# Head norms of a hybrid decoder layer: sums in quarters of the array, one root over all tokens, one product per head to spread it

## The chip, the core and the metric

The kernel runs on one core of a Trainium2 chip. A core has five engines that run side by side, each through its own list of instructions in order: TensorE (PE, with its weight loads shown apart as PEld), VectorE (DVE), ScalarE (ACT), GpSimd (POOL) and SyncE (SP, here the issuer of most DMAs). Matmul results land in PSUM, all else lives in SBUF; both have 128 partitions. The metric is the device time of one execution in microseconds (us), the median of several runs.

## The reference, cut to what matters

One decoder layer for 1024 prompt tokens and 8 sequences of 4 sample tokens: an RG-LRU branch and a gated linear attention (GLA) branch with four heads of 256 values, merged, then a SwiGLU network. What the change touches is the norm of each GLA head's output, per token, over its 256 features:

```python
o, S_T = _gla_chunked(q, k, v, g, S0)
o = o * lax.rsqrt(jnp.mean(o * o, axis=-1, keepdims=True) + EPS) * gla_norm_g.reshape(GLA_HEADS, GLA_DV)
y_b = o.reshape(B, T, GLA_DV_TOTAL) * jax.nn.silu(u_r)
m = jax.nn.sigmoid(u_ga) * (y_a @ proj_a) + jax.nn.sigmoid(u_gb) * (y_b @ proj_b)
```

All data are float32.

## The kernel before

Activations lie with features on the partitions and tokens along the free axis. The tokens are done in two halves, A (512 prompt tokens) and B (512 prompt tokens and the 32 sample tokens, 544 columns). The big products are made in float32r with each operand split in a high and a low part: `gemm` issues three matmuls per 128 features (L355, L356, L357), on pieces of 512 columns in A and of 272 in B. Weights come by DMA, are rounded to the high part on ScalarE (L136) and get their low part on VectorE (L137). Small products are plain float32 matmuls.

PSUM has two pools. `ax` (two banks) serves everything small: transposes, the sums of the norms, scores, the spreading of a norm's root. `mm` (six banks) takes the big products: six tiles of one bank in A, three of two banks in B. In SBUF the tags that matter here are "S" (17 buffers of 1088 columns) and "t" (6 buffers of 544 columns, made by `T`).

The four heads are done in two pairs. `gla(pr, ...)` makes a pair's attention: it begins with an Exp and a Ln on ScalarE (L635, L636), a scan on VectorE (L641), Exps (L646, L654), two multiplications on GpSimd (L647, L655), then masked scores (L663, L664) and seven levels of decay (L694 to L725), and ends with the squares of the pair's two heads (L839) and the sum of a head's two feature tiles into `oac` (L841), one 128 x 544 tile for each head, still to be summed over the partitions.

`head_norm(pr)` follows. In the kernel before it makes the sum over the partitions with `ssq_mm` (L362): for every 128 tokens one matmul whose stationary operand is the 128 x 128 piece of `oac` and whose moving operand is a single column of ones, so tokens come out on partitions: four pieces for each head in A, five in B. `rsqrt` (L278 to L285) computes the root on VectorE in eleven tiny instructions on 8 or 10 columns: an integer guess and three Newton steps. `spread` (L374) brings the root back along the free axis and onto all partitions, with one float32 matmul for each 128 tokens (the root's column repeated as the stationary operand, the identity as the moving one); ScalarE copies it to SBUF (L377, L379) and VectorE multiplies the head by it (L859). `y_b_tiles` (L878) and `merge_b` use the result.

The order of the work: generators yield the TensorE time of what they emit, in us, and `mix(main, fill)` emits from `fill` until it has given what `main` asked for. The emission order is a priority; a planner in the framework then fixes the order on each engine by its own estimates of durations and by when buffers come free. `head_norm(0)` runs inside `side(gla(1), head_norm(0))`: one step of it is emitted with each step of the second pair's attention, and its own yields are not used. `head_norm(1)` runs after that attention with its yields (6, 3, 3) filled from the RG-LRU branch (`lru`). In half A, chunks of the conditioning product (`ada`, L194) are woven into the fill as well; they split a product over the four 32-column quarters of the array, the way the change does:

```python
for g in range(4):
    pe.matmul(ps[32 * g:32 * g + 32, c:c + 256], cth[:, 4 * (k % 2) + g, :], raw[:, g * 256:(g + 1) * 256],
```

There are four calls of `head_norm`: A0 and A1 (half A, pairs 0 and 1), B0 and B1.

Of the kernel before, what the change touches and what calls it, by code (L numbers as in the profile page):

```python
# [7 lines left out]
F32 = mybir.dt.float32  # L8
F32R = mybir.dt.float32r
I32 = mybir.dt.int32  # L10
AF = mybir.ActivationFunctionType
OP = mybir.AluOpType
# [3 lines left out]
P = 128  # L16
# [10 lines left out]
CHUNKS = ([(0, HP)], [(0, 272), (272, 272)])  # L27
LEVELS = (64, 32, 16, 8, 4, 2, 1)
EPS = 1e-6
EARLY = 4  # L30
AHEAD = 70
def starts_of(w):
    return [min(i, w - P) for i in range(0, w, P)]
# [9 lines left out]
def bc(ap, shape):  # L43
    return ap.to_broadcast(shape)
# [3 lines left out]
def hybrid_layer(ctx, tc, I, O):  # L48
    nc = tc.nc
    pe, act, dve, pool, sp = nc.tensor, nc.scalar, nc.vector, nc.gpsimd, nc.sync  # L50
# [11 lines left out]
    cp = ctx.enter_context(tc.tile_pool(name="cp", bufs=1))  # L62
# [4 lines left out]
    tp = ctx.enter_context(tc.tile_pool(name="tp", bufs=6))  # L67
    axp = ctx.enter_context(tc.tile_pool(name="axp", bufs=2, space=PSUM))

    def S(name, dt=F32):  # L70
        return sbig.tile([P, 2 * 544], dt, tag="S", name=name)

    def T(name, w=544):
        return tp.tile([P, w], F32, tag="t", name=name)
# [15 lines left out]
    def ax(name):  # L90
        return axp.tile([P, 512], F32, tag="ax", name=name)
# [6 lines left out]
    ident = cp.tile([P, P], F32, name="ident")  # L98
# [7 lines left out]
        for t, src in (lmask, "lmask"), (bmask, "bmask"), (hlru0, "slru"), (sconv, "sconv"):  # L106
            sp.dma_start(t, I[src])
    wa2 = cp.tile([P, NH, P], F32R, name="wa2")
    ones = cp.tile([P, 1], F32, name="ones")
    pool.memset(ones, 1.0)  # L110
    rmask = cp.tile([P, 544], F32, name="rmask")
    pool.memset(rmask, 1.0)
    pool.memset(rmask[:, 0:HP:P], 0.0)
# [135 lines left out]
    def derive():  # L249
        wraw = S("wa2raw")  # L250
        w3 = wraw[:, :NH * P].rearrange("p (h m) -> p h m", m=P)
        pool.dma_start(w3, I["wa2"])
        act.activation(wa2, w3, AF.Copy)
        dve.tensor_sub(wa2[96:112], w3[96:112], wa2[96:112].bitcast(F32))
        dve.tensor_scalar_mul(vh[:, 0:20], vec[:, V_BA:V_BA + 20], 0.5)
        dve.tensor_scalar_mul(vh[:, 20:28], vec[:, V_GN:V_GN + 8], 0.5)
        lam = vec[:, V_LAM:V_LAM + NR]
        dve.scalar_tensor_tensor(lw[:, 0], lam, -1.0, lam, op0=OP.mult, op1=OP.min)
        act.activation(lw[:, 1], lw[:, 0], AF.Exp)
        dve.tensor_scalar_add(lw[:, 2], lw[:, 1], 2.0)  # L260
        dve.reciprocal(lw[:, 2], lw[:, 2])
        dve.tensor_mul(lw[:, 1], lw[:, 1], lw[:, 2])
        dve.tensor_mul(lw[:, 2], lw[:, 1], lw[:, 1])
        dve.memset(lw[:, 3], 1.0 / 17.0)
        for kk in range(7, -1, -1):
            dve.tensor_mul(lw[:, 3], lw[:, 3], lw[:, 2])
            dve.tensor_scalar_add(lw[:, 3], lw[:, 3], 1.0 / (2 * kk + 1))
        dve.tensor_mul(lw[:, 3], lw[:, 3], lw[:, 1])
        dve.tensor_scalar(lw[:, 4], lam, -1.0, 0.0, op0=OP.mult, op1=OP.max)
        dve.scalar_tensor_tensor(lw[:, 5], lw[:, 3], 2.0, lw[:, 4], op0=OP.mult, op1=OP.add)  # L270
        dve.tensor_scalar_mul(sp4, lw[:, 5], -4.0)


    def rsqrt(dst, ssq, n, scale, name):
        w = cp.tile([P, 3, 16], F32, name="rs_" + name, tag="rs", bufs=2)
        a, t = w[:, 0, :n], w[:, 1, :n]
        yi = cp.tile([P, 16], I32, name="ri_" + name, tag="ri", bufs=2)
        dve.tensor_scalar(a, ssq, scale, EPS, op0=OP.mult, op1=OP.add)  # L278
        dve.tensor_scalar(yi[:, :n], a.bitcast(I32), -0.5, float(0x5F3759DF), op0=OP.mult, op1=OP.add)
        y = yi[:, :n].bitcast(F32)  # L280
        for it in range(3):
            dve.scalar_tensor_tensor(t, a, -0.5, y, op0=OP.mult, op1=OP.mult)
            dve.tensor_mul(t, t, y)
            o = dst if it == 2 else w[:, 2, :n]
            dve.scalar_tensor_tensor(o, t, 1.5, y, op0=OP.add, op1=OP.mult)  # L285
            y = o
# [29 lines left out]
    class Half:  # L316
# [42 lines left out]

        def ssq_mm(s, ps, src, starts, col0, first, last):  # L360
            for i, o in enumerate(starts):
                pe.matmul(ps[:, col0 + i:col0 + i + 1], src[:, o:o + P], ones,  # L362
                          start=(first and i == 0), stop=(last and i == len(starts) - 1), skip_group_check=True)


# [477 lines left out]
            s.oacc = accs  # L843

        def head_norm(s, pr):
            n, N, accs = f"{s.n}{pr}", s.N, s.oacc
            os_ = s.os_[2 * pr:2 * pr + 2]
            starts = starts_of(N)
            nt = len(starts)
            ps = ax("ops" + n)  # L850
            for i in range(2):
                s.ssq_mm(ps, accs[i], starts, i * nt, i == 0, i == 1)
            rstd = cp.tile([P, 10], F32, name="orstd" + n, tag="orstd", bufs=2)
            rsqrt(rstd[:, :2 * nt], ps[:, :2 * nt], 2 * nt, 1.0 / 256, "o" + n)
            yield 6
            for i in range(2):
                rb = s.spread(rstd[:, i * nt:(i + 1) * nt], N, f"o{n}{i}")
                o3 = os_[i][:, :2 * N].rearrange("p (v n) -> p v n", v=2)
                dve.tensor_mul(o3, o3, bc(rb[:, :N].unsqueeze(1), [P, 2, N]))  # L859
                yield 3  # L860

        def r_tiles(s):
            N = s.N
# [342 lines left out]
    A.begin()  # L1206
    load_later()
    derive()
    A.branches(None)
    up1 = A.ffn1(1)  # L1210
# [115 lines left out]
```

## Time and profile before

| | us |
|---|---|
| median of 3 runs | 2040.42 (2039.70 to 2045.27) |
| the profiled execution, own time | 2041.18 |
| its span, first to last instruction | 2039.2 |
| TensorE busy | 2005.9 |
| VectorE busy | 1096.8 |
| ScalarE busy | 799.0 |
| GpSimd busy | 76.1 |

The mean granted TensorE clock of the profiled execution was 0.996. The time outside the span is 2.0 us. In a timeline, a row shows the start, the duration, the engine and line, and what was written from what; a matmul's duration includes its pipeline, so its cost is read from one row's start to the next row's start. A float32 matmul leaves two records, a float32r matmul one.

### The profile page before, as it was taken

To read this page: it belongs to the slowest core of one execution; us is meant where nothing else is said; L and a number is where in the kernel's file an instruction comes from. 1 tells how busy PE (TensorE), PEld (TensorE's weight loads), DVE (VectorE), ACT (ScalarE), POOL (GpSimd) and SP (SyncE) were. 2 spreads that over 40 slices of the span, in tenths; PEclk is the share of its full clock that TensorE was granted. 3 is DMA by queue.
4 is the path that set the end of the run, shared out by engine and by line. 5 is a ranking of instruction groups with operands and counts; after the bars stand their busy time and mean duration, and the time that the engine had idled before them with its cause. 6 is when DMAs were issued, how large, how long until landed. Compare 5 with 4: busy or idle time off the path is not lost. (4 is left out here: it accounts for less than half of the span.)

```text
span 2039.2 us, 31760 instructions
## 1 busy us (share of the span) xinstructions
PE 2005.9 (98%) x13306; PEld 1808.0 (89%) x13306; DVE 1096.8 (54%) x1768; ACT 799.0 (39%) x1117; POOL 76.1 (4%) x130
## 2 busy tenths in 40 slices
PE   8999999999999999999999999999999999999997
PEld 5887877777899888888899999999999999999997
DVE  5647586544358433446473597764334773333346
ACT  3534375533335322333352355653322442222232
POOL 0101001000000000000010011010000000000000
PEclk9999999999999999999999999999999999999998
DMA  8323223334344323232412312323233542232243
GB/s 305 105 92 125 88 94 116 102 119 159 93 153 158 124 78 119 93 132 84 149 63 87 126 53 94 109 89 104 73 92 108 177 134 87 72 105 93 82 121 123
DMA packets 74638, 228.39 MB, mean 112 GB/s; under 512 B 8704, under 2 KB 16768, under 8 KB 74496
## 3 DMA queue, kind: packets, MB, share of 16 engines
q1 hardware_dynamic: 71536, 217.38, 32.8%
q0 software_dynamic: 2416, 8.44, 1.1%
q8 instruction: 104, 1.70, 0.3%
q10 hardware_dynamic: 544, 0.56, 0.1%
q14 instruction: 38, 0.31, 0.0%
HBM read 217.11 MB, written 9.23 MB: 111 GB/s over the span
## 5 line engine op out<-in xcount | busy, mean ns | idle before, releaser
L357 PE MATMUL f3psb<-fab,f3b_hl 128*128 128x272 f32 x352 | 101.4, 288 | 0.0
L355 PE MATMUL f3psb<-fab,f3b_hl 128*128 128x272 f32 x352 | 101.3, 288 | 0.0
L356 PE MATMUL f3psb<-fab,f3b_hl 128*128 128x272 f32 x352 | 100.9, 287 | 0.0
L136 ACT ACTIVATE f3b_hl<-f3b_raw 128x768 fp32r<-128x768 f32 (+1 forms) x45 | 35.7, 793 | 88.6 <-PE f3psb L357 58.3
L355 PE MATMUL f3psa<-faa,f3a_hl 128*128 128x512 f32 x176 | 68.7, 390 | 0.0
L357 PE MATMUL f3psa<-faa,f3a_hl 128*128 128x512 f32 x176 | 68.5, 389 | 0.0
L356 PE MATMUL f3psa<-faa,f3a_hl 128*128 128x512 f32 x176 | 68.5, 389 | 0.0
L355 PEld LDWEIGHTS f3psb<-fab,f3b_hl 128*128 128x128 f32 x352 | 66.4, 189 | 0.0
L357 PEld LDWEIGHTS f3psb<-fab,f3b_hl 128*128 128x128 f32 x352 | 66.2, 188 | 0.0
L356 PEld LDWEIGHTS f3psb<-fab,f3b_hl 128*128 128x128 f32 x352 | 66.1, 188 | 0.0
L137 DVE TENSOR_TENSOR f3b_hl<-f3b_raw,f3b_hl 128x768 fp32r<-128x768 f32 (+1 forms) x45 | 40.1, 892 | 35.2 <-ACT f3b_hl L136 34.8
L136 ACT ACTIVATE f3a_hl<-f3a_raw 128x768 fp32r<-128x768 f32 (+1 forms) x32 | 25.4, 793 | 84.3 <-PE f3psa L357 47.9
L137 DVE TENSOR_TENSOR f3a_hl<-f3a_raw,f3a_hl 128x768 fp32r<-128x768 f32 (+1 forms) x32 | 28.5, 892 | 39.1 <-ACT f3a_hl L136 38.4
L355 PE MATMUL uxpsb<-h1b,uxpsb_hl 128*128 128x272 f32 x160 | 47.0, 293 | 0.1
L357 PE MATMUL uxpsb<-h1b,uxpsb_hl 128*128 128x272 f32 x160 | 46.4, 290 | 0.0
L355 PE MATMUL ugpsb<-h1b,ugpsb_hl 128*128 128x272 f32 x160 | 46.2, 289 | 0.0
L357 PE MATMUL ugpsb<-h1b,ugpsb_hl 128*128 128x272 f32 x160 | 46.1, 288 | 0.0
L356 PE MATMUL uxpsb<-h1b,uxpsb_hl 128*128 128x272 f32 x160 | 45.9, 287 | 0.0
L356 PE MATMUL ugpsb<-h1b,ugpsb_hl 128*128 128x272 f32 x160 | 45.8, 286 | 0.0
L357 PEld LDWEIGHTS f3psa<-faa,f3a_hl 128*128 128x128 f32 x176 | 33.0, 188 | 7.0 <-DVE f3a_hl L137 0.2
L356 PEld LDWEIGHTS f3psa<-faa,f3a_hl 128*128 128x128 f32 x176 | 33.0, 188 | 6.9
L355 PEld LDWEIGHTS f3psa<-faa,f3a_hl 128*128 128x128 f32 x176 | 33.0, 188 | 6.8
(1477 smaller groups left out, 7129.0 us busy)
## 6 DMA issues: line engine op xcount, KB each, us to landing
ada<-in_ada_w SPq DMA_DIRECT2D x48, 512.0 KB, 5.3
f3b_raw<-in_ffn SPq DMA_DIRECT2D x23, 384.0 KB, 3.1
f3b_raw<-in_ffn SPq DMA_DIRECT2D x22, 320.0 KB, 2.9
woa_raw<-in_w_out SPq DMA_DIRECT2D x13, 512.0 KB, 3.5
wob_raw<-in_w_out SPq DMA_DIRECT2D x13, 512.0 KB, 3.2
f3a_raw<-in_ffn SPq DMA_DIRECT2D x16, 384.0 KB, 3.1
uxpsa_raw<-in_w_in SPq DMA_DIRECT2D x10, 512.0 KB, 3.6
ugpsa_raw<-in_w_in SPq DMA_DIRECT2D x10, 512.0 KB, 3.6
```

The lines of the kernel that those rows point to most:

```text
L136: act.activation(hl[:, 0, :n], raw[:, :n], AF.Copy)
L137: dve.tensor_sub(hl[:, 1, :n], raw[:, :n], hl[:, 0, :n].bitcast(F32))
L355: pe.matmul(out, wh, x[:, o:o + w], start=st, stop=False)
L356: pe.matmul(out, wh, x[:, N + o:N + o + w], start=False, stop=False)
L357: pe.matmul(out, wl, x[:, o:o + w], start=False, stop=en)
```

## The change

The sum is turned around: a 128 x 32 block of ones is the stationary operand, and `oac` moves through the array, so the sum comes out with tokens along the free axis and repeated on 32 partitions. Four such matmuls fill the four quarters of the array: quarters 0 and 2 hold head 0, quarters 1 and 3 hold head 1. In B the 544 columns are two chunks of 272, each with an `ax` tile of its own. The root is then computed on all partitions and tokens: Ln and Exp with scale -0.5 on ScalarE give the first guess, two Newton steps follow on VectorE. The result is rounded to float32r on ScalarE, and partitions 64 to 127 get the low part. One float32r matmul for each head and chunk, with a stationary operand that picks a head's high row and low row (`pick`), adds the two parts and spreads them over all partitions. Copy and multiplication stay. `head_norm` yields 9, 1.5 and 1.5.

The new tiles: `eps` and `pick` (small constants), "on" (a buffer of tag S, with the mean square and the root), "ot" and "or" (two buffers of tag t), and in B a second `ax` tile for the sums. `ones` grows to 32 columns, and the other norms use its first column.

```diff
-    ones = cp.tile([P, 1], F32, name="ones")
+    ones = cp.tile([P, 32], F32, name="ones")
...
+    pick = cp.tile([P, 2], F32R, name="pick")
...
+        dve.tensor_add(pick, ident[:, 0:33:32], ident[:, 64:97:32])
...
-            for i in range(2):
-                s.ssq_mm(ps, accs[i], starts, i * nt, i == 0, i == 1)
-            rstd = cp.tile([P, 10], F32, name="orstd" + n, tag="orstd", bufs=2)
-            rsqrt(rstd[:, :2 * nt], ps[:, :2 * nt], 2 * nt, 1.0 / 256, "o" + n)
-            yield 6
+            chunks = CHUNKS[s.hf]
+            wt = S("on" + n)
+            a, y = wt[:, :N], wt[:, 544:544 + N]
+            pss = []
+            for ci, (o, w) in enumerate(chunks):
+                ps = ax(f"ops{n}{ci}")[:, :w]
+                for g in range(4):
+                    pe.matmul(ps[32 * g:32 * g + 32], ones, accs[g % 2][:, o:o + w], start=True, stop=True, skip_group_check=True)
+                pss.append(ps)
+            for ps, (o, w) in zip(pss, chunks):
+                act.activation(y[:, o:o + w], ps, AF.Ln, scale=1.0 / 256, bias=eps)
+                dve.tensor_scalar(a[:, o:o + w], ps, 1.0 / 256, EPS, op0=OP.mult, op1=OP.add)
+            act.activation(y, y, AF.Exp, scale=-0.5)
+            t = T("ot" + n)[:, :N]
+            for it in range(2):
+                dve.scalar_tensor_tensor(t, a, -0.5, y, op0=OP.mult, op1=OP.mult)
+                dve.tensor_mul(t, t, y)
+                dve.scalar_tensor_tensor(y, t, 1.5, y, op0=OP.add, op1=OP.mult)
+            r = tp.tile([P, 544], F32R, tag="t", name="or" + n)
+            act.activation(r[:, :N], y, AF.Copy)
+            dve.tensor_sub(r[64:, :N], y[64:], r[64:, :N].bitcast(F32))
+            yield 9
             for i in range(2):
-                rb = s.spread(rstd[:, i * nt:(i + 1) * nt], N, f"o{n}{i}")
+                rb = T(f"rbo{n}{i}")
+                for ci, (o, w) in enumerate(chunks):
+                    ps = ax(f"rpso{n}{i}{ci}")
+                    pe.matmul(ps[:, :w], bc(pick[:, i:i + 1], [P, P]), r[:, o:o + w], start=True, stop=True)
+                    act.activation(rb[:, o:o + w], ps[:, :w], AF.Copy)
                 o3 = os_[i][:, :2 * N].rearrange("p (v n) -> p v n", v=2)
                 dve.tensor_mul(o3, o3, bc(rb[:, :N].unsqueeze(1), [P, 2, N]))
-                yield 3
+                yield 1.5
```

More of the change, by code (lines that the diff above doesn't have):

```diff
@@ L108, in hybrid_layer @@
     wa2 = cp.tile([P, NH, P], F32R, name="wa2")
-    ones = cp.tile([P, 1], F32, name="ones")
+    ones = cp.tile([P, 32], F32, name="ones")
     pool.memset(ones, 1.0)
+    eps = cp.tile([P, 1], F32, name="eps")
+    pool.memset(eps, EPS)
+    pick = cp.tile([P, 2], F32R, name="pick")
     rmask = cp.tile([P, 544], F32, name="rmask")
@@ L361, in ssq_mm @@
             for i, o in enumerate(starts):
-                pe.matmul(ps[:, col0 + i:col0 + i + 1], src[:, o:o + P], ones,
+                pe.matmul(ps[:, col0 + i:col0 + i + 1], src[:, o:o + P], ones[:, 0:1],
                           start=(first and i == 0), stop=(last and i == len(starts) - 1), skip_group_check=True)
@@ L847, in head_norm @@
             os_ = s.os_[2 * pr:2 * pr + 2]
-            starts = starts_of(N)
-            nt = len(starts)
-            ps = ax("ops" + n)
-            for i in range(2):
-                s.ssq_mm(ps, accs[i], starts, i * nt, i == 0, i == 1)
-            rstd = cp.tile([P, 10], F32, name="orstd" + n, tag="orstd", bufs=2)
-            rsqrt(rstd[:, :2 * nt], ps[:, :2 * nt], 2 * nt, 1.0 / 256, "o" + n)
-            yield 6
-            for i in range(2):
-                rb = s.spread(rstd[:, i * nt:(i + 1) * nt], N, f"o{n}{i}")
+            chunks = CHUNKS[s.hf]
[20 more added lines that the diff above has]
+            yield 9
+            for i in range(2):
+                rb = T(f"rbo{n}{i}")
[3 more added lines that the diff above has]
+                    act.activation(rb[:, o:o + w], ps[:, :w], AF.Copy)
                 o3 = os_[i][:, :2 * N].rearrange("p (v n) -> p v n", v=2)
                 dve.tensor_mul(o3, o3, bc(rb[:, :N].unsqueeze(1), [P, 2, N]))
-                yield 3
+                yield 1.5
         def r_tiles(s):
```

## The prediction

> **What bounds the kernel now.** I read the page first, then the busy times by stage, then the waits and the timelines around the four calls of `head_norm`.
>
> ```profile
> PE 2005.9 (98%) x13306; PEld 1808.0 (89%) x13306; DVE 1096.8 (54%) x1768; ACT 799.0 (39%) x1117; POOL 76.1 (4%) x130
> ```
>
> TensorE is idle for only 33 of 2039.2 us. So whatever TensorE no longer does is saved, as long as it doesn't wait instead; whatever VectorE and ScalarE do more costs only where TensorE comes to wait for it. The stages that decide this are the two in which `head_norm(0)` runs beside the second pair's attention (us; PE, PEld, DVE, ACT, POOL, granted clock):
>
> ```profile
> 164.00:176.00 12.00, 8.49 (x52) 6.57 (x50) 11.53 (x11) 5.62 (x6) 6.21 (x3) 0.94 0.48 175
> 176.00:178.00 2.00, 2.00 (x12) 0.75 (x11) 1.81 (x3) 1.08 (x2) 0.00 (x0) 0.50 0.00 0
> ...
> 1163.00:1176.00 13.00, 12.98 (x104) 12.53 (x103) 12.58 (x23) 8.94 (x12) 4.16 (x3) 1.00 0.14 42
> 1176.00:1188.00 12.00, 9.70 (x86) 9.29 (x85) 12.00 (x16) 5.68 (x7) 2.62 (x2) 1.00 0.03 11
> ```
>
> VectorE is full there (11.53 of 12, then 24.6 of 25), far from its 54% over the span, and TensorE loses 3.5 and 2.3 us. What ends these waits (waits of TensorE: total, times, longest):
>
> ```profile
> PE rpsoa L374 <- DVE atta L664: 3.5, 1, 3.5
> ...
> PE spsb L710 <- DVE wb L701: 2.3, 1, 2.3
> ```
>
> Both are VectorE's. The first is a spread of A0 itself, waiting for an `ax` bank that L664 still reads. Its price is more than 3.5: the clock is 0.94 over the 12 us around it and 0.50 over the next 2, so 0.7 + 1.0 = 1.7 are lost as well, 5.2 in all. The Trainium skill ("TensorE: Matmul & The Clock Gate", Part 1: The HAM clock gate) says that TensorE falls to half its clock after an idle window of about 3.4 us. By that rule, the trace agrees (3.51 idle, then 0.50), and a wait that the change makes longer than that would cost more than itself.
>
> **What TensorE saves.** In A1 the whole of the sums and spreads can be read from one row's start to the next's:
>
> ```profile
> 272.37 1.84 PE L362 MATMUL opsa<-ones,oaca 128*128 128x1 f32 x16
> 274.07 0.49 PE L355 MATMUL uxpsa<-h1a,uxpsa_hl 128*128 128x512 f32 x1
> ...
> 279.65 1.05 PE L374 MATMUL rpsoa<-ident,orstda 128*128 128x128 f32 x8
> 280.46 0.48 PE L355 MATMUL ugpsa<-h1a,ugpsa_hl 128*128 128x512 f32 x1
> 280.77 0.39 PE L356 MATMUL ugpsa<-h1a,ugpsa_hl 128*128 128x512 f32 x1
> ...
> 292.16 0.39 PE L357 MATMUL gbpsa<-h1a,gbpsa_hl 128*128 128x512 f32 x1
> 292.39 1.02 PE L922 MATMUL g1a<-xca,lwa_raw 128*128 128x512 f32 x2
> 293.24 1.02 PE L922 MATMUL g2a<-xca,lwa_raw 128*128 128x512 f32 x2
> ```
>
> Sums 1.70, a spread 0.81, twice. The first float32r matmul behind float32 ones takes 0.31 to the next (280.46 to 280.77) where 0.23 is usual (292.16 to 292.39): 0.08 more, three times. Together 1.70 + 1.62 + 0.24 = 3.56.
>
> The new sums are four float32 matmuls of 512 columns in the four quarters. One such matmul alone takes 0.85 (292.39 to 293.24), so four in a row would be 3.4. The conditioning product already works in quarters, with 256 columns (eight records are four matmuls):
>
> ```profile
> 14.68 1.93 PE L194 MATMUL adaps<-ada,cth 128*32 128x256 f32 x32
> 17.03 1.13 PE L374 MATMUL rps1a<-ident,rstd1a 128*128 128x128 f32 x8 [0.42 <-PE adaps L194]
> ...
> 153.37 0.64 PE L194 MATMUL adaps<-ada,cth 128*32 128x256 f32 x8
> 153.94 0.50 PE L355 MATMUL vpsa<-h1a,vpsa_hl 128*128 128x512 f32 x1
> ```
>
> Four groups ended at 17.03 - 0.42 = 16.61, so one takes 0.48; a lone one takes 0.57. The quarters run side by side. For 512 columns that gives 0.96 to 1.14; I take 0.96, since the columns grow and the start-up doesn't. A spread becomes one float32r matmul, 0.23, of the kind around it. A1 after: 0.96 + 0.08 + 0.46 = 1.50, a saving of 2.1; A0 has the same instructions, so 4.1 for half A.
>
> In half B:
>
> ```profile
> 1161.90 1.17 PE L362 MATMUL opsb<-ones,oacb 128*128 128x1 f32 x10
> 1162.93 0.91 PE L663 MATMUL dpsb<-qb,kb 128*128 128x128 f32 x6
> ...
> 1296.64 1.28 PE L362 MATMUL opsb<-ones,oacb 128*128 128x1 f32 x10 [0.26 <-DVE oacb L841]
> 1298.41 1.28 PE L362 MATMUL opsb<-ones,oacb 128*128 128x1 f32 x10 [0.49 <-DVE oacb L841]
> 1299.55 1.16 PE L922 MATMUL g1b<-xcb,lwb_raw 128*128 128x272 f32 x4
> ...
> 1307.60 1.05 PE L374 MATMUL rpsob<-ident,orstdb 128*128 128x128 f32 x8
> 1308.49 0.31 PE L374 MATMUL rptob<-ident,orstdb 128*128 128x32 f32 x2
> 1308.64 0.37 PE L355 MATMUL ugpsb<-h1b,ugpsb_hl 128*128 128x272 f32 x1
> 1308.85 0.29 PE L356 MATMUL ugpsb<-h1b,ugpsb_hl 128*128 128x272 f32 x1
> 1308.97 0.29 PE L357 MATMUL ugpsb<-h1b,ugpsb_hl 128*128 128x272 f32 x1
> ```
>
> A head's sums take 1.03, its spread 1.04, and a change of kind 0.09 (0.21 against 0.12). B0: 2.06 + 2.08 + 0.3 = 4.4. After: two chunks of 0.48 x 272/256 = 0.51, a change of kind, four spreads of 0.12: 1.6. It saves 2.8. B1 is another matter: its second head's `oac` arrives only at 1298.41, and the new sums need both heads. They would end at 1298.41 + 1.02 = 1299.43, where 1299.55 stands now: a saving of 0.1. With the spreads (2.08 + 0.17 - 0.50 = 1.75) B1 saves 1.9, or 2.8 if the planner puts other matmuls ahead of the sums.
>
> Sum: 4.1 + 2.8 + 1.9 = 8.8, between 8.0 (groups at the lone price, 0.2 more in each call) and 9.7.
>
> **What the others do more.** Prices of one instruction (VectorE: 128x512, 128x544, a tiny one; ScalarE: a copy out of PSUM, a table load and what follows it):
>
> ```profile
> L841 DVE TENSOR_TENSOR oacb<-osqb 128x544 f32<-128x544 f32 x4 | 2.9, 716 | 0.0
> L841 DVE TENSOR_TENSOR oaca<-osqa 128x512 f32<-128x512 f32 x4 | 2.7, 682 | 0.1
> ...
> 274.24 0.17 DVE L278 TENSOR_SCALAR rs_oa<-opsa 128x8 f32<-128x8 f32 x1 [0.61 <-PE opsa L362]
> ...
> 279.06 0.17 DVE L285 SCALAR_TENSOR_TENSOR orstda<-rs_oa 128x8 f32<-128x8 f32 x1
> ...
> L377 ACT ACTIVATE rboa<-rpsoa x4: 585/593/598, 167.4 to 287.7; 128x512 f32<-128x512 f32 x4
> ...
> 156.62 1.28 ACT L636 ACT_TABLE_LOAD   x1
> 157.92 1.06 ACT L636 ACTIVATE ea<-ea 128x1024 f32<-128x1024 f32 x1
> ...
> L646 ACT ACT_TABLE_LOAD x4 | 5.1, 1283 | 0.1
> ```
>
> VectorE: eight full-width instructions (scale, six of Newton, low part) replace eleven of 0.17: 8 x 0.68 - 1.9 = 3.6 more in A, 8 x 0.72 - 1.9 = 3.9 in B. Queued behind them are the attention's scan, masks and levels in A0 and B0, the RG-LRU's in A1 and B1. ScalarE: Ln, Exp and rounding, 1.8 a call, and table loads of 1.28. L636 loads for Ln, and L646 loads again for Exp, so the two don't share a set here. In A0 and B0 the head's Ln can stand beside L636's and add none; in A1 and B1 it adds one or two. ScalarE is busy 39% and neither of the waits above is for it; I cost this at nothing, with the chain below as its price if the cover goes. The Trainium skill ("ScalarE: Activation LUTs", What ACT_TABLE_LOAD costs and Table sets) gives 2.66 us for a switch and names a set that holds Exp and Ln both. The trace agrees with neither: 1.28 with the next instruction right behind it (156.62 to 157.92), and two loads. By the page's figure the exposed chain below would be 2.8 longer in each call, 11 in all; the sum above wouldn't move.
>
> What hides VectorE's 3.6 and 3.9 in A0 and B0 is the fill (value and gate projections), which the planner places by readiness. It knows these instructions, so it should give TensorE other work. The bounds are 0 and 7.5, all of it waited for one to one. I take 1.0, near the lower end, because the two rows above are TensorE's long waits for VectorE in attention and `head_norm`, 5.8 in all four pairs. A gain isn't excluded either: the 5.2 of A0 hang on one moment of an `ax` bank, and may go.
>
> Sum on the profiled execution, span and outside together: 2041.18 - 8.8 + 1.0 = 2033.4. That execution lies 0.76 above the median, so **2032.6** as a median. 0.3% is 6.1 us, about what a measurement of this kernel can tell from no change: below 2034.3 is faster, above 2046.5 slower.
>
> **The rivals.**
>
> *A0's wait goes too.* The new order happens to free the bank early: 2032.6 - 5.2 = 2027.4. For it: an accident of order made it. Against: VectorE gets 3.6 more at just that place.
>
> *The saving is given back in A0 or B0.* VectorE is full there, and TensorE waits for what it does more: one place costs 3.75 - 1.0 + 1.7 of clock, 2037.1; both 2042.5. For it: 11.53 of 12 and 24.6 of 25. Against: in 1163 to 1176 VectorE was full and TensorE ran 12.98 of 13.
>
> *The quarters don't run side by side* with 512 or 272 columns: 3.4 instead of 0.96 in A, eight of 0.46 instead of 1.02 in B, 10.2 in all: 2042.8. The L194 rows speak against it.
>
> *The spread keeps its place in TensorE's list and the longer root is exposed* (slower). Alone, the chain is load, Ln, load, Exp, six, rounding, low part: 2.6 + 1.8 + 4.8 = 9.1 in A, 9.6 in B. From the last sum to the first spread there were 5.6 in A1 and 8.0 in B1 by the rows above, and in A0 and B0:
>
> ```profile
> 157.13 0.49 PE L355 MATMUL vpsa<-h1a,vpsa_hl 128*128 128x512 f32 x1
> ...
> 166.21 1.16 PE L374 MATMUL rpsoa<-ident,orstda 128*128 128x128 f32 x8
> ...
> 1165.98 1.13 PE L374 MATMUL rpsob<-ident,orstdb 128*128 128x128 f32 x8
> ```
>
> 9.1 and 3.0. So 0, 3.5, 6.6 and 1.6 are uncovered, 11.7 in all. With other work in between the chain is longer: eleven tiny instructions took from 274.24 to 279.23, 5.0 for 1.9 of work; 3.1 more in each call makes 24. In the middle, 18, with two losses of clock: 2032.6 - 1.0 + 18 + 3.4 = 2053. It decides from 15 us of such waits on. For it: `side` drops the 9 that `head_norm(0)` asks for. Against: the planner places by readiness, and A0's 9.1 were already more than its yields ask.
>
> **How the numbers follow.** Forecast 0.53, A0's wait gone 0.08, given back in one or both places 0.25, quarters in a row 0.04, chain exposed 0.10. Faster 0.61, same 0.29, slower 0.10. The range goes from 2027.4 to 2041: it leaves out the slower rival, the quarters in a row and the part of the third case with both places lost, about 0.2.
>
> **What would show it.** Sums: one group of eight records at about 1.0 in A, two of about 0.5 in B; spreads of 0.23 or 0.12; TensorE's busy time down by 7 to 9. VectorE up by about 15, ScalarE by 7 and two to four loads. If TensorE's busy time falls and its waits on spreads, L664 or L710 rise as much, the cover failed; if the sums take 3 us, the quarters did; waits over 3.5 with a clock of 0.5 behind them would show the slower case.

## The result and the profile after

The changed kernel takes 2073.69 us (median of 5 runs, 2072.19 to 2077.70); the kernel before, run beside it, 2045.27 (2039.70 to 2049.96). The ratio is 1.0146, with a 95% interval of 1.0130 to 1.0163: slower by some 28 us, where 2032.6 was forecast, and outside the range. The profiled execution took 2077.70, with a span of 2075.6 and a mean granted clock of 0.988 (before: 0.996).

The page's line of busy times, after:

```profile
PE 2013.7 (97%) x13222; PEld 1805.1 (87%) x13222; DVE 1115.5 (54%) x1759; ACT 817.3 (39%) x1139; POOL 75.0 (4%) x131
```

TensorE's busy time rose by 7.8 instead of falling. Idle time is span less busy: 33.3 before, 61.9 after, 28.6 more. The clock took 2039.2 x 0.004 = 8.2 before and 2075.6 x 0.012 = 24.9 after, 16.7 more (the clock is given to a thousandth, so about 2 either way). The two profiled executions lie 4 us on either side of the medians, so their spans differ by 36.4 and not by 28. What is left of the 36.4 is 36.4 - 28.6 - 16.7 = -8.9: TensorE has about 9 us less to do, as forecast, and loses 45 more in waits and in the slow clock behind them. The waits of TensorE after (total, times, longest):

```profile
PE rpsob L881 <- DVE orb L875: 11.3, 1, 11.3
PE rpsb L362 <- DVE rpsb_hl L141: 6.1, 1, 6.1
PE rpsoa L881 <- DVE ora L875: 4.4, 2, 3.7
...
PE pbpsa L360 <- ACT yba L174: 3.1, 1, 3.1
...
PE g1a L947 <- DVE xca L935: 2.6, 1, 2.6
```

L881 is the new spread and L875 the low part of the root, the last step of the new chain. None of these rows was among the long waits before. The stretch around each call after (A0, A1, B0, B1), then the two of pair 1 before, then two shorter ones after (us; PE, PEld, DVE, ACT, POOL, granted clock):

```profile
150.00:190.00 40.00, 34.63 (x188) 25.18 (x187) 32.40 (x40) 23.73 (x31) 5.42 (x3) 0.91 0.32 106
290.00:312.00 22.00, 15.58 (x45) 9.55 (x45) 19.74 (x30) 16.25 (x28) 0.37 (x2) 0.84 0.39 120
1165.00:1210.00 45.00, 38.79 (x290) 35.74 (x289) 38.50 (x51) 26.37 (x32) 7.85 (x6) 0.89 0.14 50
1318.00:1360.00 42.00, 29.70 (x209) 27.18 (x210) 28.88 (x45) 30.15 (x45) 2.00 (x8) 0.88 0.14 50
```

```profile
282.00:300.00 18.00, 18.00 (x78) 13.70 (x77) 17.29 (x25) 12.08 (x23) 0.00 (x0) 1.00 0.40 135
1296.00:1328.00 32.00, 31.25 (x243) 30.12 (x242) 26.76 (x50) 24.32 (x38) 3.10 (x8) 1.00 0.23 78
```

```profile
1191.00:1201.00 10.00, 6.02 (x27) 5.32 (x27) 9.36 (x14) 4.14 (x7) 0.00 (x0) 0.51 0.15 52
...
1318.00:1341.00 23.00, 10.84 (x73) 8.54 (x74) 13.32 (x21) 15.30 (x21) 0.32 (x2) 0.86 0.26 91
```

What a stretch loses is the idle time of TensorE and the length times what the clock lacks of 1. A0 loses 9.0 (5.4 + 3.6), where it lost 5.2 before; A1 9.9, where it lost nothing; B0, which lies 12 us later by now, 11.2, where it lost 2.3, with half the clock throughout 1191 to 1201; B1 17.3, where it lost 0.8. The calls of pair 1 lose 26 of the 45 more, those of pair 0 13 (before what TensorE saves, some 4 in each pair). Between 1318 and 1341 TensorE works 10.84 of 23 us, with VectorE and ScalarE not full either: three engines wait for each other.

**A1** waits less for its spreads (0.7 of the 4.4 on `ora`; the 3.7 are A0's) than for work behind the root. The product `uxpsa` was done at 280.3, and its copy (L915), which the RG-LRU's convolution needs, ran at 291.98, right behind the rounding (L874) in ScalarE's list:

```profile
291.44 0.63 ACT L874 ACTIVATE ora<-ona 128x512 fp32r<-128x512 f32 x1 [3.98 <-DVE ona L872]
```

TensorE's wait of 2.6 on L935 is for the end of that convolution.

**B1, step by step.** The timeline of ScalarE, VectorE and TensorE after; a row's bracket is the idle time ahead of it and what ended it:

```profile
1319.84 1.12 PE L862 MATMUL opsb<-oacb,ones 128*32 128x272 f32 x12 [0.67 <-DVE oacb L846]
...
1325.31 1.28 ACT L865 ACT_TABLE_LOAD   x1
1326.60 0.49 ACT L865 ACTIVATE onb<-opsb,eps 128x272 f32<-128x272 f32 x1
1327.11 1.28 ACT L955 ACT_TABLE_LOAD   x1
...
1329.81 1.28 ACT L865 ACT_TABLE_LOAD   x1
...
1332.56 1.28 ACT L867 ACT_TABLE_LOAD   x1
1333.85 0.66 ACT L867 ACTIVATE onb<-onb 128x544 f32<-128x544 f32 x1
1334.54 0.72 DVE L870 SCALAR_TENSOR_TENSOR otb<-onb 128x544 f32<-128x544 f32 x1 [0.74 <-ACT onb L867]
...
1339.10 0.66 ACT L874 ACTIVATE orb<-onb 128x544 fp32r<-128x544 f32 x1 [4.59 <-DVE onb L872]
1339.66 0.70 ACT L949 ACTIVATE trb<-g1b,vh 128x544 f32<-128x544 f32 x1
1339.78 0.72 DVE L875 TENSOR_TENSOR orb<-onb,orb 64x544 fp32r<-64x544 f32 x1 [0.72 <-ACT orb L874]
1340.65 0.79 PE L881 MATMUL rpsob<-orb,pick 128*128 128x272 f32 x2 [11.25 <-DVE orb L875]
```

From the end of the sums (1320.89) to the spread are 19.8 us, where the prediction had 9.6 for the chain alone and 12.7 with other work in between. The table load of the first Ln starts 4.4 us after the sums, behind the RG-LRU's instructions; a load for L955, which is the RG-LRU's, lies between the two Lns and makes the second one load again, so B1 has four loads. Newton then runs alone on VectorE, and ScalarE stands still for 4.59, since its next instruction is the rounding (L874). Behind that rounding in ScalarE's list wait the gates L949 and L950, which read two of B's three mm tiles; the third holds the product that TensorE finished at 1329.4.

### The profile page after: what moved, and what is told of

Same layout as the page of the kernel before. It is cut to its first block, busy times and chain, and to the rows that moved or that the text cites. A ratio compares the mean times of both kernels' runs of the same rounds, so it can differ in the third digit from the quotient of the medians.

```text
span 2075.6 us, 31617 instructions
## 1 busy us (share of the span) xinstructions
PE 2013.7 (97%) x13222; PEld 1805.1 (87%) x13222; DVE 1115.5 (54%) x1759; ACT 817.3 (39%) x1139; POOL 75.0 (4%) x131
## 5 line engine op out<-in xcount | busy, mean ns | idle before, releaser
L141 DVE TENSOR_TENSOR f3b_hl<-f3b_raw,f3b_hl 128x768 fp32r<-128x768 f32 (+1 forms) x45 | 40.1, 891 | 35.3 <-ACT f3b_hl L140 35.1
L141 DVE TENSOR_TENSOR f3a_hl<-f3a_raw,f3a_hl 128x768 fp32r<-128x768 f32 (+1 forms) x32 | 28.5, 890 | 39.0 <-ACT f3a_hl L140 38.4
L362 PE MATMUL rpsb<-h1b,rpsb_hl 128*128 128x272 f32 x128 | 37.6, 294 | 6.1 <-DVE rpsb_hl L141 6.1
L362 PEld LDWEIGHTS f3psa<-faa,f3a_hl 128*128 128x128 f32 x176 | 33.0, 188 | 7.1 <-DVE f3a_hl L141 0.2
L361 PEld LDWEIGHTS f3psa<-faa,f3a_hl 128*128 128x128 f32 x176 | 33.0, 188 | 6.9
```

What stands on the lines that cost most here:

```text
L141: dve.tensor_sub(hl[:, 1, :n], raw[:, :n], hl[:, 0, :n].bitcast(F32))
L361: pe.matmul(out, wh, x[:, N + o:N + o + w], start=False, stop=False)
L362: pe.matmul(out, wl, x[:, o:o + w], start=False, stop=en)
```

## The experiments

To compare runs made at different times, each kernel's excess over the kernel before, run beside it, is given; the change has 2073.69 - 2045.27 = +28.4. The theory C: the longer serial chain from the sums to the spread is waited for by TensorE. The rivals: V, VectorE's added load is the bound; S, the new tiles (a second ax tile, two t, one S) hold up others.

### Which pair, and which part of the chain

**e1_pair0** and **e2_pair1**: the change in one pair, the old norm (here `head_norm_old`) in the other.

```diff
-            mix(chain(iter([6]), s.head_norm(1)), fill)
+            mix(chain(iter([6]), s.head_norm_old(1)), fill)
```

> Only A0 and B0 (pair 0) use the new head norm, A1 and B1 the old one. Theory C (chain): TensorE reaches what needs the root before the longer root is there, and loses what isn't covered, most in pair 1, where the spread stood 5.6 and 8.0 us behind the sums and the fill is the RG-LRU's. In the trace after, the sums of A1 come 1.4 us later than before and the time from B0's sums to B1's is 9.4 longer, so about 11 of the 30 us: 2055. Theory V (VectorE's load): the 3.6 and 3.9 us more fall where VectorE is full, which is A0 and B0, so most of the loss is here: 2065 or more.

> Only A1 and B1 (pair 1) use the new head norm. Theory C: from A1's sums to B0's 10.6 us more, behind B1's sums 15 more in the trace after: about 20 of the 30 us, 2063. Theory V: VectorE has room there (23.1 of 25 us and 20.5 of 25 in these stretches before), so little loss, and TensorE's saving stays: 2040 or less.

Measured: 2049.38, +4.8 (ratio 1.0022, 1.0013 to 1.0032), and 2065.77, +21.2 (1.0105, 1.0084 to 1.0127). They add up to 26 of 28.4, and four fifths lie in pair 1. VectorE was full in pair 0 before; in pair 1 it was busy 23.1 of 25 us in A1 (275 to 300) and 20.5 of 25 in B1 (1300 to 1325). So V alone doesn't fit.

**e3_no_tables**: Ln and Exp become Identity with scale 0, so the root isn't computed; all else stays.

```diff
-                act.activation(y[:, o:o + w], ps, AF.Ln, scale=1.0 / 256, bias=eps)
+                act.activation(y[:, o:o + w], ps, AF.Identity, scale=0.0, bias=eps)
...
-            act.activation(y, y, AF.Exp, scale=-0.5)
+            act.activation(y, y, AF.Identity, scale=0.0, bias=eps)
```

> Ln and Exp are replaced by Identity with scale 0, which needs no table load; the root is then not computed. Same instructions and tiles otherwise. Theory C: the chain loses its loads (two in A0 that the attention needs anyway, two in A1, two more in B0, four in B1) and what waits behind them on ScalarE: at least 10 us of the 30, 2058 or less. Theory V: VectorE's work is the same, so about 2070. Theory S (buffers: two ax banks and two tiles of tag t held longer): the tiles are held 2 to 5 us shorter, 2062.

**e4_no_newton**: `range(0)` in place of `range(2)`, so the first guess is taken as it is.

> The two Newton steps (six VectorE instructions a call) and their tile are left out, so the root is only Ln's and Exp's guess; tables as in the change. Theory C: the chain is 4.1 to 4.3 us shorter in each call, 17 in all, and the loads stay: 2050 to 2055. Theory V: VectorE does no more than before (2 wide instructions for eleven tiny ones), so all of the loss goes and TensorE's saving shows: 2036 or less. Theory S: one tile of tag t less, the rest held shorter: 2055.

**e8_short**: one Identity for each bank of sums, rounding and low part; no root at all.

```diff
-                act.activation(y[:, o:o + w], ps, AF.Ln, scale=1.0 / 256, bias=eps)
-                dve.tensor_scalar(a[:, o:o + w], ps, 1.0 / 256, EPS, op0=OP.mult, op1=OP.add)
+                act.activation(y[:, o:o + w], ps, AF.Identity, scale=0.0, bias=eps)
```

> The new sums, tiles and spreads, but no root: one Identity (scale 0) from each sum's bank, the rounding and the low part; no Ln, Exp, scale or Newton. Theory C: the chain is 2 us long, about what the old root took, so TensorE's saving of 8 to 9 us shows: 2034 to 2039. Theory S (ax banks, tiles of tag t and S): the tiles are all still there, one for one except the one for Newton, so part of the loss stays: 2045 or more. If TensorE's saving were not real, 2044 as well, with TensorE's busy time as before.

Measured: without loads 2058.67, +14.1 (1.0070, 1.0051 to 1.0089); without Newton 2051.48, +6.9 (1.0035, 1.0023 to 1.0047); without the root 2040.81, -3.7 (0.9989, 0.9976 to 1.0001). So the loads are worth 14 of the 28, Newton 21, and everything in the chain 32; the first two overlap, and e4 and e8 also take work from VectorE, so only e3 speaks of the chain alone. e8_short still has the new tiles, Newton's excepted, and both ax tiles, so S has little left to explain. e3 and e8 ended 0.7 and 1.8 us above what C gave. The quarters and the single spread by themselves are no loss, but even with no chain the kernel doesn't get all of the 8.8: its span has 35.9 of idle time (33.3 before) and a clock of 0.993.

### Which engine, and how wide

**e5_int_full**: the integer guess of the old `rsqrt` and three Newton steps, all on VectorE at full width, in place of Ln, Exp and two.

```diff
-            act.activation(y, y, AF.Exp, scale=-0.5)
+            dve.tensor_scalar(yi, a.bitcast(I32), -0.5, float(0x5F3759DF), op0=OP.mult, op1=OP.add)
...
-            for it in range(2):
+            for it in range(3):
```

> The guess comes from VectorE's integer trick instead of Ln and Exp, with three Newton steps: eleven full-width VectorE instructions a call and no table load, no work on ScalarE but the rounding. Theory C: alone the chain is 11 x 0.7 + 1.3 = 9, as long as the change's 9.1 to 9.6, but without what waits behind the loads: between the run without tables (2058.7) and that plus 4 x 2.1 for the three more instructions: 2060 to 2067. Theory V: VectorE does 2.1 us more a call than in the change: 2078 or more.

**e6_half_int** and **e7_half_tab**: quarter g takes head g % 2 and token half g // 2, so that the root has 256 or 272 columns and not 512 or 544; the high and the low part then lie side by side and are added by two matmuls. e6 has the integer guess and three Newton steps, e7 Ln, Exp and two.

```diff
+            W = N // 2
...
-                    pe.matmul(ps[32 * g:32 * g + 32], ones, accs[g % 2][:, o:o + w], start=True, stop=True, skip_group_check=True)
+                pe.matmul(ps[32 * g:32 * g + 32], ones, accs[g % 2][:, (g // 2) * W:(g // 2 + 1) * W], start=True, stop=True, skip_group_check=True)
...
-                    pe.matmul(ps[:, :w], bc(pick[:, i:i + 1], [P, P]), r[:, o:o + w], start=True, stop=True)
+                        pe.matmul(o, bc(pick[:, 2 * h + i:2 * h + i + 1], [P, P]), r[:, u * W:(u + 1) * W], start=(u == 0), stop=(u == 1))
```

> Quarter g of the array takes head g mod 2 and token half g div 2, so sums, root and rounding are 256 or 272 columns wide instead of 512 or 544; integer guess and three Newton steps on VectorE; the spread takes high and low part as two float32r products of half the width each. Sums cost TensorE half (0.48, 0.51), spreads twice, the same together. Theory C: the chain is 11 x 0.40 + 0.4 + 0.4 = 5.2 and free of loads: 2 to 3 us over the old root in each call, most of it covered: 2036 to 2044. Theory V: VectorE does 3 us more a call than before, three quarters of the change's: 2058.

> As the run in token halves, but with Ln, Exp and two Newton steps as in the change. One Ln a call in B instead of two. Theory C: chain 2 loads 2.6 + 1.0 + 7 x 0.40 + 0.8 = 7.2, VectorE less than with the integer guess; loads interleaved with other functions decide: 2044 to 2052, slower than the integer guess in halves. Theory V: VectorE's extra is 1.3 us a call, the least of all with a root: 2040, faster than the integer guess in halves.

Measured: e5 2066.49, +22.0 (1.0115, 1.0084 to 1.0145), with VectorE busy 1122.8, 7.3 more than in the change, and yet nearer to the kernel before. e6 2050.75, +6.3 (1.0032, 1.0020 to 1.0044); e7 2055.30, +10.8 (1.0049, 1.0035 to 1.0063). More work for VectorE with a shorter chain is faster, which speaks against V; half the width takes most of the loss away. Both halves came out slower than C gave, e6 by 6.8 us and e7 by 3.3: a chain of half the width is not as well covered as that.

### The place of the spread

**e9_later**: the spread is emitted later.

```diff
-            yield 9
+            for _ in range(4 if pr == 0 else 0):
+                yield 0
+            yield 20 if pr else 9
```

> The change with one thing altered: the spread and what follows it are emitted later (four more steps of the second pair's attention for pair 0; for pair 1 20 us of fill are asked instead of 9). In TensorE's list B1's first spread then stands further behind the sums. Theory C (the longer root is waited for by TensorE because the spread stands too near): the waits on ora/orb (15.7 us in the changed kernel) fall below 6, and the time falls from 2073.7 by 10 to 20, to 2054 to 2064; it doesn't reach the kernel before, since ScalarE's and VectorE's lists still carry the root. A rival (the place of the spread doesn't matter: TensorE stops because the six mm banks are held by gates queued behind the root in ScalarE's and VectorE's lists): the waits only take another name, and the time stays above 2068.

**e10_half_later** and **e11_half2_later**: the same (3 steps, 16 us) for e6_half_int; e11 with two Newton steps.

> Token halves (256 or 272 columns instead of 512 or 544) with the integer guess and three Newton steps, as in e6_half_int, and the spread emitted later: three more steps in pair 0, 16 us of fill in pair 1. Theory C: e6's waits on orb (7.2) and ora (2.4) go, and with them their clock losses: 2050.8 - 9.6 - 3 = 2038, between 2034 and 2043, below the kernel before (2044.5). Rival (mm banks): within 3 us of e6, 2048 to 2054.

> As e10_half_later, with two Newton steps instead of three, so the root is less exact (about 5e-6 instead of 1e-7 relative): three VectorE instructions of about 0.40 to 0.45 less in each call, a chain shorter by 1.3. If a chain is exposed at e10 still, up to 5 us less than e10; if the chain is covered there, the same as e10 within 2 us. Theory C with e10 covered: the same.

Measured: 2071.64, +27.2 (1.0134, 1.0119 to 1.0150); 2052.46, +8.1 (1.0037, 1.0025 to 1.0050); 2056.63, +12.2 (1.0064, 1.0046 to 1.0081). C's expectation failed here, for e9 and e10 alike, and e11 came 4 us above e10, which neither side had. The waits of TensorE in e9_later:

```profile
PE rpsob L883 <- DVE orb L875: 11.2, 1, 11.2
PE rpsoa L883 <- DVE ora L875: 5.6, 1, 5.6
```

In TensorE's list of e9_later, B1's first spread stands where it stood in the change: right behind the first 48 matmuls of `uxpsb` after the sums, ahead of `ugpsb`, which the longer emission ought to have put first. Emission is only a priority; the list fits a planner that found nothing else ready at that place, which was not measured. The rival's time (above 2068) came true, but the waits kept their name. So the loss goes with the length of the chain, and asking for the spread later does not move it.

### The place of the root

From here on theory L: the root is emitted in one go ahead of the gates, so it stands ahead of them in ScalarE's and VectorE's lists, and the gates are what frees the mm tile that TensorE's next product needs. Against it D: the amount of serial work alone sets the loss.

**e12_round_dve**:

```diff
-            act.activation(r[:, :N], y, AF.Copy)
+            dve.tensor_copy(r[:, :N], y)
```

> The change with its rounding to float32r (L874) on VectorE instead of ScalarE, so that ScalarE never waits for Newton; the rest of the order is nearly the same. Theory L (gates queued behind the rounding hold the mm banks): the second gates of B1 (L949, L950) start right behind the Exp, some 5 us earlier, the products behind the spread no longer wait, and the time falls by 3 to 8 us, to 2066 to 2071; the wait on orb itself stays near 11, since the spread keeps its place. Theory D (the length of the serial chain alone): VectorE gets 0.7 more in each call and nothing is shorter, 2073 to 2077.

**e13_steps**: the root's instructions, with yields between them (Ln reads the scaled sums, so that the ax tiles come free at once; one Ln less in B).

```diff
-                act.activation(y[:, o:o + w], ps, AF.Ln, scale=1.0 / 256, bias=eps)
                 dve.tensor_scalar(a[:, o:o + w], ps, 1.0 / 256, EPS, op0=OP.mult, op1=OP.add)
+            yield 8
+            act.activation(y, a, AF.Ln)
             act.activation(y, y, AF.Exp, scale=-0.5)
+            yield 1
...
                 dve.scalar_tensor_tensor(y, t, 1.5, y, op0=OP.add, op1=OP.mult)
+                yield 1
```

> The change's own root (Ln, Exp, two Newton steps, full width), but given to the order in steps: the scale alone right behind the sums, then 8 us of other work in pair 1 (one more step of attention in pair 0), then Ln from the scaled sums and Exp, and one step more behind each of Exp and the two Newton steps. In TensorE's list B1's first spread now stands 196 matmul rows behind the sums instead of 51. Theory L: the waits on orb and ora (15.7 us in the changed kernel) fall below 4 and the time to 2048 to 2060, although ScalarE and VectorE do as much as in the change. Theory D: the work is the same, so 2066 to 2074.

**e14_half_steps** and **e15_half_mid**: the same for e6_half_int; e14 has `yield 8` behind the guess, `yield 0` behind each Newton step and the rounding on VectorE, e15 has 3, 0.5, then 6 ahead of the spread in pair 1, and the rounding on ScalarE.

> Token halves with the integer guess and three Newton steps, rounding on VectorE, and the root in steps: 8 us of other work in pair 1 (one step of attention in pair 0) behind the guess, a step behind each Newton step. B1's first spread stands 195 rows behind the sums instead of 52. Theory L: e6's waits on orb (7.2) and ora (2.4) go and their clock losses of about 3 with them: 2050.8 - 12.6 = 2038, between 2034 and 2043, below the kernel before (2044.5). Theory D: as e6, 2048 to 2054.

> As e14_half_steps with shorter distances (3 us behind the guess, 0.5 behind each Newton step, 6 ahead of the spread in pair 1) and the rounding left on ScalarE. B1's first spread stands 125 rows behind the sums. Theory L: between e6 and e14, and near e14 if 8 us was more than needed: 2036 to 2046. Theory D: as e6, 2048 to 2054.

Measured: e12 2070.77, +27.2 (1.0130, 1.0111 to 1.0148). The gates did move up; its timeline of B1:

```profile
1327.28 0.66 ACT L867 ACTIVATE onb<-onb 128x544 f32<-128x544 f32 x1
1327.85 0.70 ACT L949 ACTIVATE trb<-g1b,vh 128x544 f32<-128x544 f32 x1
...
1333.88 0.79 PE L881 MATMUL rpsob<-orb,pick 128*128 128x272 f32 x2 [11.05 <-DVE orb L875]
1334.47 0.43 PE L360 MATMUL ugpsb<-h1b,ugpsb_hl 128*128 128x272 f32 x1
```

L949 runs right behind the Exp, 5 us sooner against it than in the change, and the spread is still waited for, with the next product (ugpsb) behind it in the list. 2070.77 lies at the edge of L's range, but by the excess it is 1.2 below the change, and the two can't be told apart: freeing the tile early in fact is of no use when the list was fixed otherwise.

e13_steps 2055.80, +12.2 (1.0061, 1.0046 to 1.0076): 16 us gone with nearly the same instructions (36 table loads in ScalarE's list, 37 in the change, 29 before). Its waits:

```profile
PE vtpa L600 <- DVE atta L669: 4.9, 1, 4.9
...
PE rpsob L886 <- ACT rbob L887: 3.7, 1, 3.7
```

No wait of TensorE on `orb` or `ora` is left. B1's first spread stands behind four products of 48 matmuls, where the change had one. In ScalarE's list the gates stand ahead of the Ln:

```profile
1308.70 0.72 ACT L955 ACTIVATE tib<-g2b,vh 128x544 f32<-128x544 f32 x1 [0.16 <-PE g2b L952]
...
1315.58 0.66 ACT L867 ACTIVATE onb<-onb 128x544 f32<-128x544 f32 x1
```

e13 and e9 ask for the same 20 us of other work between B1's sums and its spread, e13 ahead of the root and between its parts, e9 behind it: the place of the root is worth 15 us of excess. e14 (17 us) against e10 (16 us) says the same with the short root, 7.4, though the rounding changed its engine there too. e14_half_steps 2044.26, +0.7 (1.0001, 0.9992 to 1.0011), e15_half_mid 2052.10, +8.5 (1.0038, 1.0024 to 1.0051). L holds for e13: D's 2066 is far off. For the short root the steps, with the rounding on VectorE, are worth 5.6 us at e14's distances; e15, for which L had 2036 to 2046, missed, and is no better than e6. e14 came out above L's 2034 to 2043 by 1 us, and its interval reaches into that range; D's 2048 is outside its interval.

### Where the rest goes

**e16_scale_act**, **e17_steps_pair1** and **e18_two_newton**: e14_half_steps with the scale of the sums on ScalarE; with the old norm in pair 0; with the scale on ScalarE and two Newton steps (a less exact root).

```diff
-            dve.tensor_scalar(a, ps, 1.0 / 256, EPS, op0=OP.mult, op1=OP.add)
+            act.activation(a, ps, AF.Identity, scale=1.0 / 256, bias=eps)
...
-            for it in range(3):
+            for it in range(2):
```

> e14_half_steps with the scale of the sums, which frees their ax bank, on ScalarE instead of VectorE. If the rest of the loss is VectorE's fullness in pair 0: the waits on L861 (1.6 and 1.2 us) go and VectorE does 0.4 less in each call, 2039 to 2042 with the kernel before at 2043.6. If it is elsewhere: 2043 to 2046.

> e14_half_steps in pair 1 alone (A1, B1), the old norm in pair 0 (A0, B0). TensorE saves 2.1 and 1.9 there by the prediction's rows. If pair 1 is now covered and pair 0 holds the rest of the loss: 2043.6 - 4 = 2039.6, between 2037 and 2042. If pair 1 still loses what it saves: 2043 to 2047.

> e16_scale_act with two Newton steps instead of three (a root exact to about 5e-6), three VectorE instructions less in each call. If VectorE's work in pair 0 holds the rest: 1 to 4 us below e16_scale_act, 2036 to 2041. If the order decides and the work does not: as e16_scale_act within 2 us, or worse by an accident of order as e11 was against e10.

Measured, 12 runs each: 2043.04, -0.7 (0.9997, 0.9987 to 1.0007); 2042.36, -1.4 (0.9992, 0.9981 to 1.0003); 2037.74, -6.0 (0.9970, 0.9959 to 0.9981). So e18_two_newton is 6 us below the kernel before and by the excesses 34 below the change, the only one with an interval wholly below 1. Its two longest waits:

```profile
PE dpssb L677 <- DVE attb L669: 3.5, 1, 3.5
PE dpsa L668 <- DVE atta L669: 3.3, 1, 3.3
```

Both are VectorE's, in pair 0 (B0 and A0). e16 has the same two rows, 3.5 and 3.3, so they do not explain the 5.3 between the two; e16's own edit took away the waits on L861 that it was meant for (1.6 and 1.2 in e14), and its time can't be told from e14's. For e18, three VectorE instructions less in each call is the only edit against e16, and where its gain comes from was not separated from an accident of order (two steps were 4 us worse in e11 than three in e10). e17's interval reaches from 1.0003 down, so the expected gain of 4 in pair 1 is not shown.

## Why the prediction was wrong, point by point

**What TensorE saves** was right in A and in sum. The rows after, A1's sums with what follows, a spread of A0 with what follows, and B0's sums:

```profile
273.74 1.07 PE L862 MATMUL opsa<-oaca,ones 128*32 128x512 f32 x8
274.74 0.50 PE L360 MATMUL uxpsa<-h1a,uxpsa_hl 128*128 128x512 f32 x1
...
185.37 0.39 PE L881 MATMUL rpsoa<-ora,pick 128*128 128x512 f32 x1
185.60 0.40 PE L361 MATMUL rpsa<-h1a,rpsa_hl 128*128 128x512 f32 x1
...
1169.62 1.10 PE L862 MATMUL opsb<-oacb,ones 128*32 128x272 f32 x4
1170.65 0.39 PE L360 MATMUL rpsb<-h1b,rpsb_hl 128*128 128x272 f32 x1
...
1173.22 1.12 PE L862 MATMUL opsb<-oacb,ones 128*32 128x272 f32 x12
1174.27 0.39 PE L361 MATMUL rpsb<-h1b,rpsb_hl 128*128 128x272 f32 x1
```

The sums took 1.00 (0.96 taken, 3.4 if the quarters had run in a row) and the spread 0.23. B0's sums were split by the planner: two of head 0 went first, one behind the other, and took 1.03, the other six 1.05, so 2.08 and no saving on the sums there, where 1.0 had been counted. That takes the 8.8 to 7.8; the account of the span gives 8.9.

**What the others do more.** VectorE's 18.7 (about 15 forecast) was near. ScalarE rose by 18.3, not by 7 and two to four loads: its list has eight loads more. The prediction counted none for A0 and B0 and one or two for A1 and B1, as if Ln and Exp stood together. In the trace L865 loads four times, L867 three times, L893 and L955, which came in between, once each, and L651 once less.

**The step that failed** is the cover: "It knows these instructions, so it should give TensorE other work", costed at 1.0, and asked for in A0 and B0 only, with ScalarE's share "at nothing" because it is busy 39%. None of this holds. A1 and B1, which the sum left out without a reason, hold four fifths of the loss (e2, +21.2). In B1 the planner gave TensorE no other work. Shown is that moving the root, and not the spread, takes the wait away (e13 against e9). That what held the other work was an mm tile, which the gates behind the root would have freed, fits the lists and is argued, not shown: e12 freed it sooner and gained nothing, since the list of TensorE stayed. And an engine that is idle 61% of the span still is a place in line: L874 kept it for 4.59 us in B1 and 3.98 in A1. The whole chain, with no root left, is worth 32 us (e8), against the 1.0 taken.

**The rivals.** The slower one, with 0.10, came true as a mechanism in B1 and was too small: 18 of waits and 3.4 of clock against 28.6 and about 16.7. It also had the places wrong. It gave B1 1.6 uncovered, which became 11.3, A0 nothing, which became 3.7, and A1 3.5, which became 0.7. It gave B0 6.6; B0's spread was not waited for, and instead a weight's low part (L141) came 6.1 late, behind four Newton instructions among others on VectorE:

```profile
1182.03 2.52 POOL L652 TENSOR_TENSOR qeb<-qb,e0b 128x1088 f32<-128x1088 f32 x1 [12.11 <-ACT e0b L651]
1182.46 2.68 DVE L870 SCALAR_TENSOR_TENSOR otb<-onb 128x544 f32<-128x544 f32 x1 [0.84 <-ACT onb L867]
1186.50 3.02 POOL L660 TENSOR_TENSOR keb<-keb,kb 128x1088 f32<-128x1088 f32 x1 [1.95 <-ACT keb L659]
1187.69 2.41 DVE L870 SCALAR_TENSOR_TENSOR otb<-onb 128x544 f32<-128x544 f32 x1
...
1193.71 1.21 DVE L141 TENSOR_TENSOR rpsb_hl<-rpsb_raw,rpsb_hl 128x1024 fp32r<-128x1024 f32 x1
...
1194.98 0.59 PE L362 MATMUL rpsb<-h1b,rpsb_hl 128*128 128x272 f32 x1 [6.10 <-DVE rpsb_hl L141]
```

Its reason, that `side` drops the 9, does not bear either: e9 gave those steps and more, and A0 and B0 were not the bulk. "Given back in A0 or B0" (0.25) looked at the calls where VectorE is full, and four fifths of the loss came in pair 1, where it had some room (e1, e2). "The planner places by readiness" was used against the slow case; if it is so, it is why the spread stayed.

**Open.** Why the planner held B1's spread to be the next thing ready was not measured; the order of TensorE's list up to A1's spreads is the same with the loads and without them (e3), which fits a planner that does not count them. Of the 8 to 9 us saved on TensorE, e18 keeps 6; where the rest of e14's goes is not settled.

## What to carry to other kernels

Before a short step on a narrow tile is traded for a longer one on other engines, write down the serial time from the last producer to the first consumer, with the table loads that other functions in between will cause, and ask what stands behind each of its instructions in each engine's list; an engine's low share of the span says nothing on that. If a consumer is waited for, and emitting it later does not move it, look for the resource that the other work needs (here, by the lists, an mm tile) and for what holds that back; emit the producer in steps behind it. And keep the serial part narrow: half the columns were worth 17.6 us of excess here (e7, with Ln, Exp and two Newton steps as in the change, but one Ln less in B), where no edit at full width that computes the root in one go was worth more than 6.4 (e5).

## What the runs showed of the hardware

**The half clock after short idles.** The same place of the network's first product in both kernels: the timeline and the stretch behind it (granted clock third from the end) after the change, then the same two views before:

```profile
1662.91 0.39 PE L360 MATMUL f1psb<-h2b,f1b_hl 128*128 128x272 f32 x1 [0.45 <-ACT h2b L439]
1663.95 0.39 PE L361 MATMUL f1psb<-h2b,f1b_hl 128*128 128x272 f32 x1 [0.64 <-DVE h2b L440]
1664.71 0.36 PE L360 MATMUL f2psb<-h2b,f2b_hl 128*128 128x272 f32 x1 [0.24 <-DVE fxwb L1069]
```

```profile
1666.00:1670.00 4.00, 4.00 (x23) 4.00 (x23) 1.54 (x5) 1.08 (x2) 0.00 (x0) 0.62 0.13 48
```

```profile
1628.19 0.39 PE L355 MATMUL f1psb<-h2b,f1b_hl 128*128 128x272 f32 x1 [0.45 <-ACT h2b L434]
1629.23 0.39 PE L356 MATMUL f1psb<-h2b,f1b_hl 128*128 128x272 f32 x1 [0.64 <-DVE h2b L435]
```

```profile
1632.00:1636.00 4.00, 4.00 (x34) 3.79 (x32) 2.68 (x6) 2.61 (x4) 0.00 (x0) 1.00 0.02 5
```

Two idles of 0.45 and 0.64 left the clock at 1.00 before; with a third of 0.24 close behind them it was 0.62 over the 4 us from 1666. The change doesn't touch this place, and every run has the two idles, so its twenty traces can be compared. In the five with these two alone the clock stayed at 1.00. With a third one it fell to 0.50 for at least 2 us in nine, and stayed at 1.00 in six: where the third took 0.62, 0.80, 0.92 and 0.99 (e12, e14, e5, e7), and where 0.23 came ahead of the two (e1, e2). So short idles can cost the clock, and neither their number nor their sum decides whether they do; what does is not shown. The Trainium skill ("TensorE: Matmul & The Clock Gate", Part 1: The HAM clock gate) has the fall come after an idle window of about 3.4 us; the rows above show it after idles that add up to 1.33, none longer than 0.64.

**VectorE beside GpSimd.** In the rows of B0 above, a Newton instruction of 128 x 544 took 2.68 beside GpSimd's L652, where the same one took 0.72 in B1. GpSimd's instruction ended at 1184.55, and 0.59 later VectorE's did. The second, of 2.41 beside L660, ended 0.58 behind it. Before, one instruction of another kind (L695) was caught so in B0, for 2.69; now it is two of the new chain. The Trainium skill ("SBUF — State Buffer", Terms) says that the two arbitrate for one pair of ports, which one of them holds for a whole instruction while the other is blocked; these rows agree: what is left behind GpSimd's end, 0.59 and 0.58, is most of one instruction of 0.72.
